# Operands for the second half made inside the first MLP, decode pages multiplied in halves, and wider spacing of memory-key steps

## The chip, the cores and the metric

The kernel runs on one core of a Trainium2 chip. The metric is device time in microseconds of one execution. The engines named below are TensorE (PE in the profile, with PEld for its weight loads), VectorE (DVE), ScalarE (ACT), GpSimd (POOL, which also issues DMAs) and the DMA issuing queue of SyncE (SP).

## What is computed

One inference step of a one-layer decoder, in fp32, for two groups of rows that share the weights: a prompt of 1024 rows and 8 sample rows that each attend to 8192 cached positions. Cut to what matters here:

```python
# prompt
q, k, v, logf, u, z = mixer_inputs(rmsnorm(xp, g_mix), w_in, b_f, g_sgu_v)
xp = xp + merge_heads(fox_prompt(q, k, v, logf), sgu_prompt(u, z, w_s, b_s), g_att_out, g_sgu_out, w_o)
mk, mv = memory_kv(mem_prompt, g_mem, w_ck, w_cv)                  # 256 memory rows
xp = xp + cross_attend(rmsnorm(xp, g_cross), mk, mv, w_cq, w_co)
xp = xp + conv_ffn(rmsnorm(xp, g_ffn), 0, w_up, conv_w, conv_b, w_down)[0]
# samples: the same, with
att = fox_sample(q, k, v, logf, cache_k, cache_v, cache_logf, page_table)   # 64 pages of 128 rows each
xs = xs + cross_attend(rmsnorm(xs, g_cross), cache_mem_k, cache_mem_v, w_cq, w_co)
# merge_heads: concatenate([rmsnorm(att), rmsnorm(sgu)]) @ w_o
# conv_ffn: h = x @ w_up; width-3 causal convolution over rows; (silu(gate) * val) @ w_down, 2816 columns each
```

## The kernel before

**Matmuls.** Every fp32 operand is split into a high and a low part of a faster matmul type (`split`, L231-236): ACT writes the high part (L232, or L235 with a scale), DVE the low part (L233, or L236). `gemm3` (L269-271) then issues three matmuls for each product. Weights arrive by SP DMAs into `wr` tiles of 512 KB (4 buffers) and are split into `wh` (5 buffers) and `wl` (4). Activations lie in a pool `u` of 18 tiles of 128 x 1024. PSUM has eight banks: four `ba`, two `bb`, one `ms`, one `dv`. The prompt's tiles rotate over `ba` and `bb`, every third on `bb`; the samples use `ms` and `dv`.

**The prompt.** The 1024 rows go through in two halves of 512. The order is: projections, attention of half 0, attention of half 1, then for half 0 and then for half 1: a middle stage ("mid0", "mid1") and an MLP ("ffn0", "ffn1"), then the final norm. The middle stage has three parts. `merge_in` (L908) loads the normed attention and gating rows, and `merge` makes their transposed, scaled and split operands in 8 steps: 4 transposes into a bank (L880), then one split by ACT and DVE. `out_proj` (L960) multiplies with `w_o` and adds into the residual rows (`residual`, L952, a DVE add from PSUM and a square on ACT). Cross-attention begins and the MLP begins with `norm_T` (L1018), which transposes three of the four row blocks first (L1027, split in pieces of 128 x 384) and the fourth later (L1043, pieces of 128 x 128).

The MLP (`ffn`, L1167) works in groups of columns. A group first runs its up-projection tiles: 24 matmuls each, a scaled copy by ACT, two convolution steps by DVE (L1214, L1215), in the second half of the prompt a fix of two columns (L1217), and for each pair a product (L1221) and its split. Then it runs down-projection tiles: for each of two column halves (n = 0, 1) and four row blocks. The last group of `ffn` ends with four such tiles at n = 1, and its residual rows are complete after them. A hook, `late`, is called before the last group's down-projection; in half 0 it only issues the loads of `merge_in(1)`.

**The samples.** A second program runs beside the prompt. `decode` goes through 8 samples. For each it takes 16 key steps (`kstep`: an indirect DMA issued by POOL that gathers 1 MB of key pages into a `kv` tile, L1326, a DVE multiply by the query, L1332, and a DVE reduction, L1336) and 16 value steps (`vstep`, L1385: the value pages, then PE matmuls into `dv`, L1391). There are four `kv` tiles. In the attention phases of the prompt a page's multiply and reduction are cut in `KS` = 2 halves, elsewhere each is one instruction of 128 x 2048. Then `sample_rest` follows: the output projection (`sample_proj`, weights through `kv` tiles, sums in bank `ms`), a norm, the query projection, the cross-attention to each sample's own memory keys (a loop over 8 samples: two broadcast loads of the query, a 1 MB load, two multiplies, L1555, one reduction, L1556), to its memory values, and the samples' MLP.

**What sets the order.** Both programs are Python generators. The prompt yields an estimate of its PE time; the driver at the end adds it up and advances the samples' generator by one step each time the sum has passed `PACE` of the phase (8 in mid0, 8.5 in ffn0, 6.8 in mid1, 2.5 in ffn1, 2.9 for `sample_rest`), unless `held[0]` is set. The instructions so issued are then ordered for each engine by a scheduler with its own estimate of times. Two tools steer it: `behind(engine)` places instructions after the last one of the prompt on that engine, and `tc.high_priority()` puts them ahead. The order of an engine is fixed in the built program; what varies in an execution is only how long each instruction waits.

Of the kernel before, what the change touches and what calls it, by code (L numbers as in the profile page):

```python
# [12 lines left out]
ALU = mybir.AluOpType  # L13
AX = mybir.AxisListType
PSUM = bass.MemoryType.PSUM
ENG = mybir.EngineType
DRAM = bass.MemoryType.DRAM

P = 128
# [10 lines left out]
FF = 2816  # L30
NF = FF // P
NPAGE = 64
EPS = 1e-6
NEG = -1e30
UW = 1024
# [43 lines left out]
def build(nc, tc, ctx, a, phases=None):  # L79
# [1099 lines left out]
    def ffn(hf, xt, ys, late=None):  # L1179
        w0, pv0 = wload(a["w_up"][0], 1024), BK()  # L1180

        def up(out, w, hs, ls, c):
            hv, lv = (w[q].rearrange("p (k c) -> p k c", c=P) for q in range(2))
            gemm3(out, [(hv[:, k, :], lv[:, k, :], hs[k][:, c], ls[k][:, c]) for k in range(8)])

        hs, ls = yield from norm_T(ys, G_FFN, lambda hs, ls, c: up(pv0[:, c], w0, hs, ls, c))
        if hf:

            fix = sm([P, 2 * NF, 2], "fix", 1)
            tap = [gp[:, CW + i * 44 : CW + i * 44 + 44] for i in range(2)]  # L1190
            for c in range(2):
                nc.vector.tensor_tensor(fix[:, :, c], hlast[0][:, :, 1], tap[1 - c], op=ALU.mult)
            t = sm([P, 2 * NF], "fixt", 1)
            nc.vector.tensor_tensor(t, hlast[0][:, :, 0], tap[0], op=ALU.mult)
            nc.vector.tensor_tensor(fix[:, :, 0], fix[:, :, 0], t, op=ALU.add)
        sq = squares()
        f0 = 0
        for gi, gn in enumerate(GROUPS):
            gh, gl = [], []
            for f in range(f0, f0 + gn):  # L1200
                hc2 = []
                for part in range(2):
                    ft = f + part * NF
                    cw = [gp[:, CW + i * 44 + ft : CW + i * 44 + ft + 1] for i in range(3)]
                    cb = gp[:, CB + ft : CB + ft + 1]
                    if ft:
                        w_, pv = wload(a["w_up"][ft], 1024), BK()
                        up(pv, w_, hs, ls, slice(0, 512))
                    else:
                        pv = pv0  # L1210
                    hc = T2()
                    nc.scalar.activation(hc, pv, AF.Identity, bias=cb, scale=cw[2])
                    nc.scalar.activation(hlast[hf][:, ft, :], pv[:, 510:512], AF.Copy)
                    nc.vector.scalar_tensor_tensor(hc[:, 1:], pv[:, :511], cw[1], hc[:, 1:], op0=ALU.mult, op1=ALU.add)  # L1214
                    nc.vector.scalar_tensor_tensor(hc[:, 2:], pv[:, :510], cw[0], hc[:, 2:], op0=ALU.mult, op1=ALU.add)  # L1215
                    if hf:
                        nc.vector.tensor_tensor(hc[:, 0:2], hc[:, 0:2], fix[:, ft, :], op=ALU.add)  # L1217
                    hc2.append(hc)
                    yield 5.2
                nc.scalar.activation(hc2[0], hc2[0], AF.Silu)  # L1220
                nc.vector.tensor_tensor(hc2[1], hc2[1], hc2[0], op=ALU.mult)  # L1221
                q = (f - f0) % 2
                if q == 0:
                    g2, l2 = U([P, 2, 512], F32R), U([P, 2, 512], F32R)
                split(hc2[1], g2[:, q, :], l2[:, q, :])
                gh.append(g2[:, q, :])
                gl.append(l2[:, q, :])
            if late and f0 + gn == NF:
                late()
            for n in range(2):  # L1230
                ws = []
                for k2 in range(0, gn, 2):
                    m = min(2, gn - k2)
                    r0 = (f0 + k2) * P
                    h, l, _ = wload(
                        a["w_down"][r0 : r0 + m * P, n * 512 : (n + 1) * 512].rearrange("(k p) n -> p k n", p=P), m * 512
                    )
                    for q in range(m):
                        ws.append((h[:, q, :], l[:, q, :]))
                for i in range(4):  # L1240
                    tb = slice(i * P, (i + 1) * P)
                    ps = MM()
                    gemm3(ps[:, :512], [(gh[k][:, tb], gl[k][:, tb], ws[k][0], ws[k][1]) for k in range(gn)])
                    if f0 + gn < NF:
                        xs_ = xt[i][:, n * 512 : (n + 1) * 512]
                        nc.vector.tensor_tensor(xs_, ps[:, :512], xs_, op=ALU.add)
                    else:
                        residual(xt, sq, i, n, ps)
                    yield 3.9
            f0 += gn  # L1250
        if hf:
            nc.sync.dma_start(a["o_h"], hlast[1])
        return sq
# [20 lines left out]
    def decode():  # L1274
# [48 lines left out]
        def kstep(b, ch, st):  # L1323
            qb, s = st
            kv = KV()
            nc.gpsimd.indirect_dma_start(kv, None, a["cache_k"], off(kidx[:, b, ch : ch + 1]))  # L1326
            kvv = kv.rearrange("p (k c) -> p k c", c=512)
            sp = KS if phase[0][:3] == "att" else 1
            m = 4 // sp
            with behind(ENG.DVE):  # L1330
                for i in range(0, 4, m):
                    nc.vector.tensor_tensor(  # L1332
                        kvv[:, i : i + m, :], kvv[:, i : i + m, :], qb.unsqueeze(1).broadcast_to((P, m, 512)), op=ALU.mult
                    )
                for i in range(0, 4, m):
                    nc.vector.tensor_reduce(  # L1336
                        s[:, ch * 4 + i : ch * 4 + i + m, :].rearrange("p k h -> p (k h)"),
                        kvv[:, i : i + m, :].rearrange("p k (h d) -> p (k h) d", d=64),
                        axis=AX.X,
                        op=ALU.add,  # L1340
                    )
# [138 lines left out]
    def sample_out(n, ps, fin):  # L1480
        t = D2()
        nc.scalar.activation(t, ps, AF.Copy)
        yield 1
        ps2 = MS()
        mmul(ps2[:8, :], selS, t, start=True, stop=True)
        fin(n, ps2[:8, :])

    def sample_proj(w, xT, fin):
        for n in range(2):
            ps = MS()  # L1490
            for kk in range(4):
                if kk % 2 == 0:
                    raw = KV().rearrange("p (k n) -> p k n", n=512)
                    nc.gpsimd.dma_start(raw, w[kk * 256 : (kk + 2) * 256, n * 512 : (n + 1) * 512].rearrange("(k p) n -> p k n", p=P))
                    yield 1
                sample_mm(ps, raw[:, (kk % 2) * 2 : (kk % 2) * 2 + 2, :], kk, xT, 512)
            yield from sample_out(n, ps, fin)

    def sample_rest(xs):
        yield 1  # L1500
# [45 lines left out]
        for b in range(8):  # L1546
            qb = [D2(), D2()]
            for n in range(2):
                nc.gpsimd.dma_start(qb[n], q2s_d[b : b + 1, n * 512 : (n + 1) * 512].broadcast_to((P, 512)))
            kv = KV()  # L1550
            nc.gpsimd.dma_start(kv.rearrange("p (a c) -> p a c", c=D), a["cmk"][b].rearrange("(a p) c -> p a c", p=P))
            kvv = kv.rearrange("p (a c) -> p a c", c=D)
            for n in range(2):
                kn = kvv[:, :, n * 512 : (n + 1) * 512]
                nc.vector.tensor_tensor(kn, kn, qb[n].unsqueeze(1).broadcast_to((P, 2, 512)), op=ALU.mult)  # L1555
            nc.vector.tensor_reduce(sS[:, :, b, :], kv.rearrange("p (a h d) -> p a h d", a=2, h=4), axis=AX.X, op=ALU.add)  # L1556
            yield 1
        yield 1
        tr = MS()
        for mt in range(2):  # L1560
# [160 lines left out]
    def prompt():  # L1721
# [2 lines left out]
            if not G0R:  # L1724
                yield from gating(0)

        got = []
        att1 = attention(1, lambda: got.append(merge_in(0)))
        att0, fill0 = attention(0, (lambda: next(att1)) if LT < 4 else None, LT), fill()

# [27 lines left out]
        next(ending)  # L1758
        ends = []
        for hf in range(2):  # L1760
            if not got:
                got.append(merge_in(hf))
            xt = []
            phase[0] = f"mid{hf}"
            mh, ml = yield from beside(merge(*got.pop()), ending, (3, 7)) if hf == 0 else merge(*got.pop())
            if ends:
                yield from ends.pop()
            sq = yield from out_proj(a["w_o"], mh, ml, xt, partial(load_x, hf))
# [2 lines left out]
            else:  # L1771
                ys = yield from cross(xt, sq)
            phase[0] = f"ffn{hf}"
            sq = yield from ffn(hf, xt, ys, (lambda: got.append(merge_in(1))) if LM and hf == 0 else None)
            ends.append(final(hf, xt, sq))
        yield from ends.pop()

# [8 lines left out]
    for t in prompt():  # L1786
# [8 lines left out]
        while bgs and not held[0] and most and acc[0] >= PACE[phase[1] or phase[0]]:  # L1795
            most -= 1
            acc[0] -= PACE[phase[1] or phase[0]]
            if next(bgs[0], None) is None:
                bgs.pop()
        seen = len(nc.cur_bb.bb.instructions)  # L1800
    for _ in bgs.pop() if bgs else ():
        pass
# [90 lines left out]
```

## Time and profile before

| | |
|---|---|
| median of 3 runs | 1905.01 us (1898.7 to 1908.0) |
| the profiled execution | 1899.86 us, its span 1898.1 us |
| PE busy | 1817.0 us (96%), 9255 matmuls |
| VectorE busy | 1394.5 us (73%), 1574 instructions |
| ScalarE busy | 755.7 us (40%) |
| GpSimd busy | 490.6 us (26%) |
| moved by DMA | 517.06 MB, mean 272 GB/s |
| mean granted TensorE clock | 0.979 |

The profile's times count from the start of the span. The middle stage of half 0 lies around 545 to 780 us, its MLP from there to 1166, the middle stage of half 1 from 1166 to about 1410, and its MLP from there to the end. The loop over the samples' memory keys lies at 1573 to 1635. "Idle before" is the time an engine sat with nothing to do ahead of an instruction, and the name behind the arrow is what ended that time.

### The profile page before, as it was taken

To read this page: it belongs to the slowest core of one execution; us is meant where nothing else is said; L and a number is where in the kernel's file an instruction comes from. 1 tells how busy PE (TensorE), PEld (TensorE's weight loads), DVE (VectorE), ACT (ScalarE), POOL (GpSimd) and SP (SyncE) were. 2 spreads that over 40 slices of the span, in tenths; PEclk is the share of its full clock that TensorE was granted. 3 is DMA by queue.
4 is the path that set the end of the run, shared out by engine and by line. 5 is a ranking of instruction groups with operands and counts; after the bars stand their busy time and mean duration, and the time that the engine had idled before them with its cause. 6 is when DMAs were issued, how large, how long until landed. Compare 5 with 4: busy or idle time off the path is not lost.

```text
span 1898.1 us, 24082 instructions
## 1 busy us (share of the span) xinstructions
PE 1817.0 (96%) x9255; PEld 1299.4 (68%) x9255; DVE 1394.5 (73%) x1574; ACT 755.7 (40%) x1371; POOL 490.6 (26%) x429
## 2 busy tenths in 40 slices
PE   8999999788899999999999999998999999999998
PEld 5987666555676667777767776775675667667765
DVE  4888678776678786989989998888764548754344
ACT  5332356565633534424233243325353333232332
POOL 1342242222122332313431322344222012101110
PEclk9999999989999999999999999999999999999999
DMA  8867988853397875869878879888859557666872
GB/s 320 292 246 278 324 319 292 280 168 126 136 376 251 337 274 214 310 229 353 307 266 311 309 298 348 340 337 300 308 218 356 198 200 271 226 223 255 323 275 101
DMA packets 156371, 517.06 MB, mean 272 GB/s; under 512 B 20168, under 2 KB 41928, under 8 KB 123488
## 3 DMA queue, kind: packets, MB, share of 16 engines
q0 software_dynamic: 56400, 339.04, 48.0%
q1 hardware_dynamic: 92944, 163.89, 24.8%
q10 hardware_dynamic: 6912, 12.59, 1.8%
q8 instruction: 73, 1.20, 0.2%
q14 instruction: 42, 0.34, 0.0%
HBM read 493.63 MB, written 21.84 MB: 272 GB/s over the span
## 4 chain that ended last, share of the span: by engine, by line
PE 82%; DVE 8%; ACT 4%; DMA 3%; issue 2%; POOL 0%; SPq 0%; DVEq 0%; POOLq 0%; ACTq 0%
PE ba L270 12%; PE ba L269 12%; PE ba L271 12%; PE bb L269 7%; PE bb L270 7%; PE bb L271 7%; PE dv L1391 6%; DVE kv L1332 2%; DMA kv<-cache_k,kidx 1%; PE dv L1634 1%; PE bb L795 1%; PE ba L993 1%; PE ba L994 1%; PE ba L995 1%; DVE wl L233 1%
## 5 line engine op out<-in xcount | busy, mean ns | idle before, releaser
L232 ACT ACTIVATE wh<-wr 128x1024 fp32r<-128x1024 f32 (+2 forms) x220 | 228.7, 1044 | 483.0 <-PE ba L270 154.6
L233 DVE TENSOR_TENSOR wl<-wr,wh 128x1024 fp32r<-128x1024 f32 (+2 forms) x220 | 262.6, 1200 | 155.4 <-PE ba L271 70.2
L1326 POOL DMA_INDIRECT kv<-cache_k,kidx x128 | 185.7, 1451 | 528.6 <-DVE s L1336 241.7
L1332 DVE TENSOR_TENSOR kv<-kv,d 128x2048 f32<-128x2048 f32 (+1 forms) x139 | 292.4, 2114 | 34.9 <-DMA kv<-cache_k,kidx 34.0
L1336 DVE TENSOR_REDUCE s<-kv 128x32 f32<-128x2048 f32 (+1 forms) x139 | 292.2, 2106 | 0.7
L1385 POOL DMA_INDIRECT kv<-cache_v,kidx x128 | 182.5, 1426 | 403.5 <-DVE s L1336 196.1
L269 PE MATMUL ba<-wh,u 128*128 128x512 f32 (+1 forms) x596 | 227.0, 382 | 0.0
L270 PE MATMUL ba<-wl,u 128*128 128x512 f32 (+1 forms) x596 | 226.2, 380 | 0.0
L271 PE MATMUL ba<-wh,u 128*128 128x512 f32 (+1 forms) x596 | 223.1, 379 | 0.7 <-DVE u L233 0.7
L269 PE MATMUL ba<-u,wh 128*128 128x512 f32 (+2 forms) x520 | 203.6, 392 | 1.2 <-DVE u L236 1.2
L270 PE MATMUL ba<-u,wh 128*128 128x512 f32 (+2 forms) x520 | 204.1, 393 | 0.0
L271 PE MATMUL ba<-u,wl 128*128 128x512 f32 (+2 forms) x520 | 202.9, 390 | 0.0
L1391 PE MATMUL dv<-kv,s 128*32 128x512 f32 x1024 | 138.2, 614 | 5.5 <-DMA kv<-cache_v,kidx 5.5
L269 PE MATMUL bb<-u,wh 128*128 128x512 f32 (+2 forms) x344 | 137.7, 400 | 0.0
L270 PE MATMUL bb<-u,wh 128*128 128x512 f32 (+2 forms) x344 | 136.4, 397 | 0.0
L271 PE MATMUL bb<-u,wl 128*128 128x512 f32 (+2 forms) x344 | 135.4, 395 | 0.0
L269 PEld LDWEIGHTS ba<-wh,u 128*128 128x128 f32 x596 | 112.5, 189 | 31.9 <-issue 8.0
L271 PEld LDWEIGHTS ba<-wh,u 128*128 128x128 f32 x596 | 111.8, 188 | 28.6 <-issue 6.3
L270 PEld LDWEIGHTS ba<-wl,u 128*128 128x128 f32 x596 | 112.5, 189 | 24.6 <-issue 3.8
L270 PEld LDWEIGHTS ba<-u,wh 128*128 128x128 f32 x520 | 98.7, 190 | 32.8 <-issue 12.6
L269 PEld LDWEIGHTS ba<-u,wh 128*128 128x128 f32 x520 | 98.8, 190 | 31.8 <-issue 7.1
L271 PEld LDWEIGHTS ba<-u,wl 128*128 128x128 f32 x520 | 98.6, 190 | 28.5 <-issue 9.3
(416 smaller groups left out, 3080.5 us busy)
## 6 DMA issues: line engine op xcount, KB each, us to landing
wr<-w_up SPq DMA_DIRECT2D x88, 512.0 KB
kv<-w_up POOLq DMA_DIRECT2D x22, 1024.0 KB
wr<-w_down SPq DMA_DIRECT2D x40, 512.0 KB
kv<-w_down POOLq DMA_DIRECT2D x11, 1024.0 KB
wr<-w_in SPq DMA_DIRECT2D x16, 512.0 KB
wr<-w_o SPq DMA_DIRECT2D x16, 512.0 KB
wr<-w_cq SPq DMA_DIRECT2D x16, 512.0 KB
wr<-w_co SPq DMA_DIRECT2D x16, 512.0 KB
```

What stands on the lines that cost most here:

```text
L232: nc.scalar.activation(h, src, AF.Copy)
L233: nc.vector.tensor_tensor(l, src, h.bitcast(F32), op=ALU.subtract)
L269: mmul(out, sh, mh, start=(i == 0), stop=False)
L270: mmul(out, sh, ml, start=False, stop=False)
L271: mmul(out, sl, mh, start=False, stop=(i == n - 1))
L795: mmul(po[64 * j : 64 * j + 64, q0:256], vn[:, kt, 64 * j : 64 * j + 64], pt[j][kt // 4][:, kt % 4, q0:256], start=(kt == 0), stop=(kt == ...
L993: mmul(pss[i], mh[k][:, tb], wh, start=(k == korder[0]), stop=False)
L1326: nc.gpsimd.indirect_dma_start(kv, None, a["cache_k"], off(kidx[:, b, ch : ch + 1]))
L1332: nc.vector.tensor_tensor(kvv[:, i : i + m, :], kvv[:, i : i + m, :], qb.unsqueeze(1).broadcast_to((P, m, 512)), op=ALU.mult)
L1336: nc.vector.tensor_reduce(s[:, ch * 4 + i : ch * 4 + i + m, :].rearrange("p k h -> p (k h)"), kvv[:, i : i + m, :].rearrange("p k (h d) -> ...
L1385: nc.gpsimd.indirect_dma_start(kv, None, a["cache_v"], off(kidx[:, b, ch : ch + 1]))
L1391: mmul(dv[32 * j : 32 * j + 32, :], s[:, ch * 4 : ch * 4 + 4, :].rearrange("p k h -> p (k h)"), kvv[:, j, :], start=(ch == 0), stop=(ch == ...
```

## The change

Five things change.

1. The hook `late` of `ffn` in half 0 now returns the generator `merge(1)` (its loads are issued at the same place as before). After each of the four last down-projection tiles (last group, n = 1) two of its 8 steps are run. From the first of these on `held[0]` is set, so the samples' program rests until `ffn` returns. Half 1 then takes the finished operands and goes straight on to the final norm of half 0 and to `out_proj`.
2. A page's multiply and reduction are cut in halves in mid0 and mid1 too.
3. `sample_proj` uses bank `dv` for its first column half and `ms` for the second, and issues both halves' matmuls before either half's sums.
4. The loop over memory keys puts its DVE instructions `behind(DVE)`, cuts the reduction in two, and yields `CMK` = 3 instead of 1; the driver charges that step three times.
5. The load of `merge_in(hf)` at the head of the loop is limited to half 0.

In the new file lines from the MLP's hook on stand one to some twenty lines further down (L880 becomes L881).

```diff
+CMK = 3
...
+            side = None
             if late and f0 + gn == NF:
-                late()
+                side = late()
...
                     yield 3.9
+                    if side and n:
+
+                        held[0] = True
+                        for _ in range(2):
+                            yield next(side)
...
-            sp = KS if phase[0][:3] == "att" else 1
+            sp = KS if phase[0][:3] in ("att", "mid") or held[0] else 1
...
-        ps2 = MS()
+        ps2 = (DV, MS)[n]()
...
     def sample_proj(w, xT, fin):
+        outs = []
         for n in range(2):
-            ps = MS()
+            ps = (DV, MS)[n]()
...
-            yield from sample_out(n, ps, fin)
+            outs.append(sample_out(n, ps, fin))
+            next(outs[n])
+        for o in outs:
+            yield from o
+        yield 1
...
-            for n in range(2):
-                kn = kvv[:, :, n * 512 : (n + 1) * 512]
-                nc.vector.tensor_tensor(kn, kn, qb[n].unsqueeze(1).broadcast_to((P, 2, 512)), op=ALU.mult)
-            nc.vector.tensor_reduce(sS[:, :, b, :], kv.rearrange("p (a h d) -> p a h d", a=2, h=4), axis=AX.X, op=ALU.add)
-            yield 1
+            with behind(ENG.DVE):
+                for n in range(2):
+                    kn = kvv[:, :, n * 512 : (n + 1) * 512]
+                    nc.vector.tensor_tensor(kn, kn, qb[n].unsqueeze(1).broadcast_to((P, 2, 512)), op=ALU.mult)
+                for i in range(2):
+                    nc.vector.tensor_reduce(sS[:, i, b, :], kvv[:, i, :].rearrange("p (h d) -> p h d", h=4), axis=AX.X, op=ALU.add)
+            yield CMK
...
-            if not got:
+            if not got and hf == 0:
...
-            mh, ml = yield from beside(merge(*got.pop()), ending, (3, 7)) if hf == 0 else merge(*got.pop())
+            if hf == 0:
+                mh, ml = yield from beside(merge(*got.pop()), ending, (3, 7))
+            else:
+                mh, ml = yield from ahead[0]
...
-            sq = yield from ffn(hf, xt, ys, (lambda: got.append(merge_in(1))) if LM and hf == 0 else None)
+            sq = yield from ffn(hf, xt, ys, (lambda: ahead.append(merge(*merge_in(1))) or ahead[0]) if hf == 0 else None)
+            held[0] = False
...
-            if next(bgs[0], None) is None:
+            w = next(bgs[0], None)
+            if w is None:
                 bgs.pop()
+            else:
+                acc[0] -= (w - 1) * PACE[phase[1] or phase[0]]
```

More of the change, by code (lines that the diff above doesn't have):

```diff
@@ L1725, in fill @@
                 yield from gating(0)
-        got = []
+        got, ahead = [], []
         att1 = attention(1, lambda: got.append(merge_in(0)))
```

## The prediction

> **What bounds the kernel now.** I read the page first, then the PE waits, then windows over the places where PE waited.
>
> ```profile
> span 1898.1 us, 24082 instructions
> PE 1817.0 (96%) x9255; PEld 1299.4 (68%) x9255; DVE 1394.5 (73%) x1574; ACT 755.7 (40%) x1371; POOL 490.6 (26%) x429
> PE 82%; DVE 8%; ACT 4%; DMA 3%; issue 2%; POOL 0%; SPq 0%; DVEq 0%; POOLq 0%; ACTq 0%
> ```
>
> PE is busy for 1817.0 of 1898.1 us, and 82% of the chain that ended last is PE. So 81 us of idle PE, start and end included, is nearly all that a change of order can win, beside matmuls that ran at a lowered clock. The PE waits say for whom PE sat idle (us in total, times, longest):
>
> ```profile
> PE bb L269 <- DVE t L1217: 6.4, 1, 6.4
> PE dv L1391 <- DMA kv<-cache_v,kidx: 5.5, 2, 3.6
> PE ba L880 <- DVE u L952: 3.8, 1, 3.8
> PE ba L1043 <- DVE u L236: 3.8, 2, 1.9
> PE ba L1027 <- DVE u L236: 3.3, 2, 2.2
> PE bb L1027 <- DVE u L952: 2.9, 2, 2.5
> ```
>
> In the second half of the kernel PE mostly waits for VectorE, and in single pieces of 2 to 6 us. The windows place them. Columns: us, then busy time of PE, PEld, DVE, ACT and POOL (instructions), the granted clock, DMA share, GB/s.
>
> ```profile
> 586.20:588.30 2.10, 0.24 (x2) 0.12 (x1) 2.10 (x5) 0.00 (x0) 0.00 (x0) 0.93 0.36 152
> 588.00:591.40 3.40, 3.22 (x12) 2.86 (x13) 3.40 (x5) 0.63 (x2) 0.00 (x0) 0.50 0.03 5
> 1169.90:1173.90 4.00, 0.20 (x3) 0.07 (x2) 4.00 (x6) 2.45 (x7) 2.47 (x2) 1.00 1.03 414
> 1175.00:1178.50 3.50, 3.50 (x19) 2.63 (x12) 3.50 (x5) 1.59 (x3) 0.94 (x1) 0.51 0.99 372
> 1231.70:1240.50 8.80, 5.71 (x35) 5.09 (x32) 8.80 (x13) 2.28 (x5) 3.52 (x2) 1.00 0.95 381
> 1310.90:1323.00 12.10, 6.50 (x23) 3.45 (x21) 8.95 (x10) 5.85 (x17) 1.88 (x2) 0.72 0.95 381
> 1610.20:1616.80 6.60, 0.22 (x2) 0.13 (x1) 6.60 (x8) 1.14 (x2) 0.71 (x1) 0.89 0.84 295
> 1616.00:1622.50 6.50, 5.80 (x14) 4.64 (x15) 6.50 (x9) 1.17 (x2) 0.00 (x0) 0.52 0.55 209
> ```
>
> Read them in pairs. From 1169.90 to 1173.90 DVE is busy without pause while PE does 0.20 us, and from 1175.00 the clock is 0.51 for 3.5 us. The pair at 1610 is the largest: PE does 0.22 of 6.60 us, then runs at 0.52 for another 6.5 us. A gap of under 2 us near 587 is followed by the same 0.50, while the two gaps inside 1231.70 to 1240.50 leave the clock at 1.00. So a lost microsecond of PE can cost up to two.
>
> [...]
>
> **The change part by part.** *Memory-key steps of the samples* (spacing of three, held behind DVE's last main instruction, reductions in halves). This stretch now:
>
> ```profile
> 1577.00:1632.00 55.00, 47.87 (x195) 37.96 (x194) 54.93 (x56) 16.43 (x26) 10.49 (x17) 0.94 0.76 262
> L1555 DVE TENSOR_TENSOR kv<-kv,d 128x1024 f32<-128x1024 f32 x16 | 19.3, 1218 | 4.7 <-DMA d<-q2s_d 4.7
> L1556 DVE TENSOR_REDUCE sS<-kv 128x8 f32<-128x2048 f32 x8 | 18.2, 2277 | 0.0
> L233 DVE TENSOR_TENSOR wl<-wr,wh 128x1024 fp32r<-128x1024 f32 x9 | 10.9, 1216 | 0.0
> L1214 DVE SCALAR_TENSOR_TENSOR t<-ba,gp,t 128x511 f32<-128x511 f32 x4 | 3.0, 743 | 0.0
> L1221 DVE TENSOR_TENSOR t<-t,t 128x512 f32<-128x512 f32 x4 | 2.7, 684 | 0.0
> ```
>
> DVE is full for 55 us. Its own 24 instructions take 19.3 + 18.2 = 37.5 us, about 36 at the spacing of starts (a record overlaps the next by some 0.08). An up-projection tile asks DVE for a weight split (1.14 by starts), two convolution steps (0.66 each), a small fix, and half of a gate product and its split (0.60 each): about 3.1 us. Seven such tiles and two weight splits for the next group make 36 + 22 + 2 = 60 us of DVE. Seven tiles are 7 x 24 matmuls, 0.23 us apart (starts 1159.64, 1159.86, 1160.09 below), so 39 us of PE. DVE falls 21 us behind. PE sat idle for 55 - 47.87 = 7.1 of it, so buffers absorbed about 14. After the change eleven tiles stand between the first and the last memory-key step: DVE 36 + 11 x 3.1 = 70, PE 11 x 5.5 = 61. The 9 us of lag left is below the 14 that buffers absorbed. What can go is 7.1 of gap and the lowered clock behind it, 14 matmuls in 5.80 us at 1616, 0.41 each instead of 0.23: 2.6: together 9.7. I take -8.5, since at the turn from up- to down-projection tiles the margin is only about 1 us. Bounds: -10 (all), and 0 if the lag just moves there. The cover for the decode steps is PE's lead; if it is gone, the same 7 us come back. Splitting eight reductions adds 8 x 0.07 = 0.6 of DVE, inside the lag. The steps come later, but the steps after them take up the delay: behind the samples' last DVE instruction stand 24 of the prompt's, where 19 stood, so the end isn't lengthened.
>
> *Second half's operands between the last down tiles of the first MLP.*
>
> ```profile
> 1156.61 0.69 DVE L952 TENSOR_TENSOR u<-ba,u 128x512 f32<-128x512 f32 x1
> 1157.22 2.28 DVE L1332 TENSOR_TENSOR kv<-kv,d 128x2048 f32<-128x2048 f32 x1
> 1159.42 0.68 DVE L952 TENSOR_TENSOR u<-ba,u 128x512 f32<-128x512 f32 x1
> 1160.02 0.68 DVE L952 TENSOR_TENSOR u<-bb,u 128x512 f32<-128x512 f32 x1
> 1168.57 2.27 DVE L1336 TENSOR_REDUCE s<-kv 128x32 f32<-128x2048 f32 x1
> 1170.76 2.35 DVE L233 TENSOR_TENSOR wl<-wr,wh 128x1024 fp32r<-128x1024 f32 x2
> 1173.09 0.68 DVE L952 TENSOR_TENSOR u<-ba,u 128x512 f32<-128x512 f32 x1
> 1159.64 0.39 PE L269 MATMUL ba<-wh,u 128*128 128x512 f32 x1
> 1159.86 0.39 PE L270 MATMUL ba<-wl,u 128*128 128x512 f32 x1
> 1160.09 0.39 PE L271 MATMUL ba<-wh,u 128*128 128x512 f32 x1
> ```
>
> Today PE reaches the transposes at 1169.9 and waits 3.80 us for a residual add (L952) that stands on DVE behind a page reduction and two weight splits. The same 32 transposes, 32 scalings and residual adds are issued afterwards; none is saved. In pairs of four they now stand between tiles of 15 matmuls (3.5 us of PE), in which ACT and DVE split them. That cover holds for the later pairs. The first pair needs a bank that a residual add frees. In the new DVE order that add stands behind another add and a full page multiply: starts 0.61 + 2.20 + 0.60 apart, 3.4 us, against about 1.4 of PE work in front of it by the new PE order (two matmuls and a group of page matmuls, an estimate), so a new wait of about 2.0; the last tile may wait 0.8 for its add, a little more than one add takes. So 3.80 goes and 2.8 comes; with the lowered clock at 1175 gone (3.5 us at half rate, of which I count 1.3 as lost), and a half chance of 1.5 for a drop behind the new wait, that is -1.0 - 1.3 + 0.75 = -1.5. Bounds: -5 (both stalls gone) and +2 (both new waits with a clock drop, no old cost saved but half). On SP, three loads of the output projection's weights now stand behind g_final and four x loads; those wait for buffers that PE's tiles free. At 1169.9 DMA share is 1.03, so a late load is possible; I cost it at 0, hidden behind the remaining tiles, and up to +2 without that cover. Decode is held for about 16 us of yielded work, and afterwards goes on one step per main step until it has caught up; its instructions are in the same places again before cross-attention. Price 0; if not, see the second rival.
>
> *Pages in halves in the mid stages.* 45 more pages become four instructions.
>
> ```profile
> L1332 DVE TENSOR_TENSOR kv<-kv,d 128x2048 f32<-128x2048 f32 x117 | 266.6, 2283 | 34.9 <-DMA kv<-cache_k,kidx 34.0 <-PE bb L1126 0.7
> L1332 DVE TENSOR_TENSOR kv<-kv,d 128x1024 f32<-128x1024 f32 x22 | 25.8, 1215 | 0.0
> 1235.56 2.28 DVE L1336 TENSOR_REDUCE s<-kv 128x32 f32<-128x2048 f32 x1
> 1237.75 2.28 DVE L1332 TENSOR_TENSOR kv<-kv,d 128x2048 f32<-128x2048 f32 x1
> 1240.03 0.60 DVE L236 SCALAR_TENSOR_TENSOR u<-ba,gp,u 128x128 fp32r<-128x128 f32 x2
> ```
>
> Two halves take 2 x 1215 - 2283 = 147 ns more by duration; by starts about 0.07 per pair, two pairs a page: 45 x 0.14 = 6 us more DVE work over the two mid stages. It costs PE nothing unless DVE is awaited. Halves only help if something is ordered between them. In the new order, at the waits near 575, 586 and 737, the two halves still stand together ahead of the awaited scaling, so these stay. Near 1238 the multiply of 2.28 us, which stood ahead of the scalings at 1240.03, now stands behind the first two: the 1.9 us wait ends 2.2 us earlier and goes. Take -2. Bounds: -8 (every one of those waits halved, with its clock drop) to +4 (each of about five gets 0.14 to 0.3 longer, and one more drop).
>
> *Samples' projections* (two PSUM buffers in turn): PE has no wait in these stretches now, so 0, within 1 either way.
>
> Sum: -8.5 - 1.5 - 2 = -12.0 on the profiled execution's 1899.86, so 1887.9. That execution is 5.15 below the median of 1905.01; on the median I forecast 1893.0.
>
> **The rivals.** (a) *The samples' lag moves rather than goes.* The memory-key steps run on into the turn to the down-projection, where DVE must free banks for tiles of fewer matmuls; about 7 us of idle PE return and the parts above give only 3: 1905 - 12 + 8.5 = 1901.5. For it: margin of 1 us there, DVE at 54.93 of 55. Against: 14 us absorbed now.
>
> (b) *Slower: pages late in the second mid stage.* The one wait of this kind now is in the row from 1310.90: PE does 6.50 of 12.10 us at a clock of 0.72, so 5.6 idle and some 2.6 slowed, 8 us for one late V page. Holding decode for 16 us and then issuing a step at each main step bunches page loads where DMA share is already 0.95 to 1.03. Each such page beyond today's adds 8 to the 1893: one gives 1901, two 1909, three 1917. From the second on the change loses; I price the rival at three, 1917. Against it: the queues' order of page loads is nearly the same, and PE waited for cache_v only twice in the whole execution (the second row of the waits).
>
> (c) *That late V page disappears.* Ahead of it stands a long POOL issue:
>
> ```profile
> 1294.47 0.94 POOL L1385 DMA_INDIRECT kv<-cache_v,kidx  x1 [0.30 <-PE ba L1100]
> 1296.46 9.07 POOL L1326 DMA_INDIRECT kv<-cache_k,kidx  x1 [1.05 <-DVE s L1336]
> ```
>
> Its neighbour took 0.94 us. If DVE's work beside it held it up, shorter DVE instructions may let it through, and then the 8 us go too: 1885. [...]
>
> (d) *The halves do nothing*, since the planner keeps them adjacent: 1895; part of my forecast's range.
>
> **How the numbers follow.** Forecast 0.47 (alone 1887 to 1899), (a) 0.19, (b) 0.18, (c) 0.16. A difference under 0.5% (9.5 us) is about what measurement can't tell from none. Faster by more: all of (c) and four fifths of the forecast, 0.54. Within: (a) and the rest of the forecast, 0.28. Slower: (b) at three pages or more, 0.18. The range of 8 in 10 runs from 1881, (c) with its bounds, to 1910, past (a) and up to two late pages of (b).
>
> **What would show it.** The 6.4 us wait of L269 for t L1217 should be gone, with the clock at 1.00 there, and the memory-key steps spread over some 60 to 75 us. The transposes of L880 (L881 then) should stand between tiles, with one PE wait near 2 us before them in place of 3.80. The waits at 575, 586 and 737 should be as before; that near 1238 should be gone. I am wrong if PE's waits for DMA in the second mid stage grow, if a wait of 3 us or more appears at the MLP's turn, or if PE's idle time falls by 12 us and the span doesn't.

## The result and the profile after

The changed kernel takes 1883.97 us (median of 7 runs, 1881.13 to 1890.86) where the kernel before takes 1904.38 us (7 runs, 1895.84 to 1909.6). The ratio is 0.9903, with a 95% interval of 0.9884 to 0.9923: 15 to 22 us faster. In a later comparison it was 0.9929 (0.9913 to 0.9945). The two profiled executions differ by less, 1899.86 against 1887.23 us. The head of the page of after:

```profile
span 1885.5 us, 24204 instructions
PE 1810.9 (96%) x9255; PEld 1298.5 (69%) x9255; DVE 1400.3 (74%) x1672; ACT 755.7 (40%) x1371; POOL 478.6 (25%) x429
PE 84%; DVE 6%; DMA 4%; ACT 3%; issue 2%; POOL 1%; SPq 0%; DVEq 0%; POOLq 0%; ACTq 0%
```

VectorE does 6 us more work, as the halves ask (1400.3 against 1394.5). PE's busy time falls by 6 us with the same 9255 matmuls; fewer of them at a lowered clock would do that (behind the 6.38 us wait of before they start 0.43 us apart, at full clock 0.23), but the mean granted clock of the two executions, 0.979 and 0.980, is too coarse to show it. PE's waits in after (us in total, times, longest), the ones that answer to the list before:

```profile
PE dv L1398 <- DMA kv<-cache_v,kidx: 5.5, 2, 3.6
...
PE ba L1028 <- DVE u L237: 5.0, 4, 2.2
...
PE bb L1028 <- DVE u L953: 3.3, 2, 2.5
PE ba L270 <- DVE u L953: 2.7, 2, 2.5
...
PE bb L1044 <- DVE u L237: 2.2, 1, 2.2
...
PE bb L271 <- DVE u L237: 1.5, 1, 1.5
```

The wait of 6.4 us for t L1217 is gone. The 3.8 us before the transposes is gone, and a wait of 2.5 for a residual add (L953 now) has come. The waits of norm_T and the matmuls behind it for the scalings (L237) did not shrink: 5.0, 2.2 and 1.5 us here, 3.8 and 3.3 in the rows before. Two windows of after, columns as in the prediction:

```profile
1550.00:1612.00 62.00, 62.00 (x271) 50.59 (x270) 61.87 (x75) 22.31 (x40) 10.49 (x18) 1.00 0.73 249
1174.00:1178.50 4.50, 4.50 (x26) 2.93 (x25) 4.50 (x7) 3.85 (x6) 2.56 (x1) 1.00 0.85 294
```

In the first, which holds most of the memory-key loop of after (1550.6 to 1617.8), DVE is as full as before (61.87 of 62) and PE does not pause once, at full clock. The second lies behind the new 2.53 us wait: the clock stayed at 1.00.

### The profile page after: what moved, and what is told of

The parts are those of the page before. It is cut to its first block, busy times and chain, and to the rows that moved or that the text cites. A ratio compares the mean times of both kernels' runs of the same rounds, so it can differ in the third digit from the quotient of the medians.

```text
span 1885.5 us, 24204 instructions
## 1 busy us (share of the span) xinstructions
PE 1810.9 (96%) x9255; PEld 1298.5 (69%) x9255; DVE 1400.3 (74%) x1672; ACT 755.7 (40%) x1371; POOL 478.6 (25%) x429
## 4 chain that ended last, share of the span: by engine, by line
PE 84%; DVE 6%; DMA 4%; ACT 3%; issue 2%; POOL 1%; SPq 0%; DVEq 0%; POOLq 0%; ACTq 0%
PE ba L270 13%; PE ba L271 13%; PE ba L272 12%; PE bb L270 7%; PE bb L271 7%; PE bb L272 7%; PE dv L1398 6%; DVE kv L1339 1%; PE dv L1648 1%; DVE s L1343 1%; PE bb L796 1%; PE ba L994 1%; PE ba L996 1%; PE ba L995 1%; DMA wr<-w_ck 1%
## 5 line engine op out<-in xcount | busy, mean ns | idle before, releaser
L1339 DVE TENSOR_TENSOR kv<-kv,d 128x1024 f32<-128x1024 f32 (+1 forms) x184 | 295.5, 1634 | 27.3 <-DMA kv<-cache_k,kidx 27.1
L1333 POOL DMA_INDIRECT kv<-cache_k,kidx x128 | 175.0, 1367 | 552.8 <-DVE s L1343 257.6
L1343 DVE TENSOR_REDUCE s<-kv 128x16 f32<-128x1024 f32 (+1 forms) x184 | 296.6, 1626 | 0.2
L270 PE MATMUL ba<-wh,u 128*128 128x512 f32 (+1 forms) x601 | 229.7, 384 | 3.1 <-DVE u L953 2.7
L270 PE MATMUL ba<-u,wh 128*128 128x512 f32 (+2 forms) x520 | 204.4, 394 | 0.4 <-DVE u L237 0.4
L270 PE MATMUL bb<-u,wh 128*128 128x512 f32 (+2 forms) x344 | 138.6, 403 | 0.7 <-DVE u L237 0.7
L270 PEld LDWEIGHTS ba<-wh,u 128*128 128x128 f32 x601 | 113.3, 189 | 37.6 <-issue 10.7
L270 PEld LDWEIGHTS ba<-u,wh 128*128 128x128 f32 x520 | 99.3, 191 | 31.4 <-issue 8.4
```

The costliest lines, as they stand in the source:

```text
L270: mmul(out, sh, mh, start=(i == 0), stop=False)
L1339: nc.vector.tensor_tensor(kvv[:, i : i + m, :], kvv[:, i : i + m, :], qb.unsqueeze(1).broadcast_to((P, m, 512)), op=ALU.mult)
L1343: nc.vector.tensor_reduce(s[:, ch * 4 + i : ch * 4 + i + m, :].rearrange("p k h -> p (k h)"), kvv[:, i : i + m, :].rearrange("p k (h d) -> ...
```

## The experiments

**How the stages are read.** Single traces carry noise: from the start to the fifth residual add the built order is the same in the ten kernels whose pages are whole in mid0, and yet this stretch took 551.4 to 557.4 us in their traces. (In the four with halves in mid0 a few pages of this stretch are already in halves; they took 555.4 to 558.1.) So I cut each trace at four instructions of the prompt: the fifth residual add (L952), the first convolution step of the first MLP (L1214), its 41st, and the first convolution step of the second MLP; the last cut is the last scaling of the final norm. Kernels with the same edit in a stage stand together. In mid0, in the first MLP and, where the table does not say otherwise, around mid1 their orders of instructions are the same, so they are replicas; in the second MLP they differ in places. All numbers in us, from the starts of those instructions:

| stage | edit in force there | traces | time, mean | lowest to highest |
|---|---|---|---|---|
| mid0 | pages whole | 10 | 206.3 | 205.5 to 207.4 |
| | pages in halves | 4 | 209.8 | 209.1 to 211.5 |
| first MLP, to its 41st up tile | any | 14 | 358.2 | 358.2 to 358.3 |
| from there through mid1 | merge behind the MLP, whole | 4 | 299.4 | 298.2 to 300.1 |
| | merge behind, halves (two orders) | 2 | 299.1 | 298.6 to 299.5 |
| | merge inside, decode held, whole | 2 | 295.6 | 295.2 to 296.0 |
| | merge inside, held, halves in mid0 and mid1 | 3 | 293.3 | 291.6 to 295.8 |
| | merge inside, held, halves in mid1 only | 2 | 290.2 | 289.3 to 291.1 |
| | merge inside, not held, halves in mid1 only | 1 | 287.7 | |
| second MLP | loop and projections as before | 3 | 477.6 | 477.4 to 478.0 |
| | loop alone changed | 1 | 476.3 | |
| | projections alone changed | 1 | 475.8 | |
| | both, spacing of one | 1 | 474.4 | |
| | both changed | 8 | 467.2 | 465.1 to 469.5 |

The changed kernel is by this +3.5 in mid0, -6.1 around mid1 and -10.4 in the second MLP: -13.0. The second measured ratio is -13.5 us, the first -18.5.

**The memory-key loop alone.** To the kernel before (the comments stand for lines of the change that are left out here):

```diff
+CMK = 3
-            for n in range(2):                 # two multiplies, one reduction
+            with behind(ENG.DVE):              # two multiplies, two half reductions
...
-            yield 1
+            yield CMK
...
+            else:
+                acc[0] -= (w - 1) * PACE[phase[1] or phase[0]]
```

> The kernel before with one part of the change alone: the loop over memory keys spaced by three, its DVE instructions held behind the prompt's, its reductions in halves. My theory (the lag of DVE is absorbed by PE's lead): the wait of 6.4 us of L269 for t L1217 goes with its lowered clock, 9 to 11 us faster, ratio 0.994 to 0.9955. Rival (the lag moves to the turn to the down-projection tiles): a wait of 4 us or more appears there, at most 3 us faster, ratio 0.998 or more.

Measured: 0.9985 (0.9971 to 0.9998), so 0.4 to 5.5 us, and the rival's number. The wait is still there. First a row of its PE waits, then a window over it:

```profile
PE bb L270 <- DVE t L1218: 5.1, 1, 5.1
```

```profile
1612.00:1626.00 14.00, 8.86 (x30) 6.77 (x29) 14.00 (x17) 2.97 (x5) 1.27 (x2) 0.76 0.71 274
```

The built order tells why: between the first and last step still lie seven up tiles, as before, and the loop still ends at the turn to the down-projection. The spacing could not stretch it. My theory, that this edit alone gives room, falls.

**The samples' projections alone, and both.** To the kernel before (the second kernel has the edit above as well):

```diff
-            ps = MS()
+            ps = (DV, MS)[n]()
...
-            yield from sample_out(n, ps, fin)
+            outs.append(sample_out(n, ps, fin))
+            next(outs[n])
+        for o in outs:
+            yield from o
+        yield 1
```

> The kernel before with the samples' projections alone changed (two PSUM banks in turn, both halves' matmuls first); the memory-key loop as before. By the built order the loop then starts three up tiles earlier in its MLP group and has four up tiles behind it before the turn, in place of none, and six between its steps in place of seven. Theory L (the place of the loop decides: the lag is paid back before the turn): the wait of 6.4 us goes without any spacing, ratio 0.994 to 0.996. Theory S (the spacing decides too): 21 us of lag in six tiles are still more than the buffers absorb, a wait of 4 us or more stays earlier in the group, ratio 0.998 to 1.000.

> The kernel before with the projections and the memory-key loop both changed, nothing else. By the built order ten up tiles lie between the first and the last step. Both theories: the wait goes, ratio 0.993 to 0.9955; theory L expects no difference to the projections alone, theory S 6 us or more between them. If it gains less than 4 us, the rest of the change is needed too and both fall.

The projections alone: 0.9994 (0.9978 to 1.001), no difference. Both: 0.9951 (0.9932 to 0.997). Theory S has the right ratios and L falls, though the wait of 4 us or more that S placed earlier in the group did not come: two edits that are each worth 1 to 2 us in the second MLP's stage are worth 10 together. With the projections alone the loop starts at 1556.8 in place of 1572.1, PE goes through it without a pause, and the loss comes behind it. Two windows, and PE's timeline (start, busy time, then idle before and who ended it):

```profile
1556.00:1607.00 51.00, 51.00 (x223) 41.61 (x222) 50.84 (x52) 17.54 (x31) 10.47 (x18) 1.00 0.79 268
1607.00:1630.00 23.00, 19.23 (x71) 14.31 (x70) 21.70 (x35) 11.34 (x18) 1.43 (x2) 0.85 0.58 211
```

```profile
1616.40 0.40 PE L1566 MATMUL ms<-cp,sS 128*32 128x128 f32 x2 [2.08 <-DVE sS L1561]
1618.19 0.79 PE L269 MATMUL bb<-wh,u 128*128 128x512 f32 x1 [1.40 <-DVE t L1215]
```

The steps are issued closely, so the samples' own transposes of the finished scores (L1566) stand in PE's order before VectorE has worked off the reductions, and PE waits for them with all up tiles behind; then the lag shows as a second wait. With the spacing as well, the same loop spreads over 1551.0 to 1621.1, ten up tiles instead of six:

```profile
1551.00:1616.00 65.00, 65.00 (x284) 52.96 (x283) 64.97 (x81) 24.09 (x41) 11.03 (x18) 1.00 0.75 257
```

DVE is full, and so is PE. The traces show a second thing that the projections change. In the four kernels without that edit DVE itself sits idle for 4.4 to 5.4 us before steps at the head of the loop, until the loads of the query land (2.16 and 2.56 us in the kernel before); in the ten with it this takes 0.4 us at most. How much of the pair's gain is this and how much the earlier start, no run separates.

**The spacing back to one in the changed kernel.**

```diff
-CMK = 3
+CMK = 1
```

> The changed kernel with the memory-key steps spaced by one again (still behind DVE's main work and in halves). Theory L: same as the changed kernel within 2 us, ratio to before 0.990 to 0.992. Theory S: 5 us or more slower than the changed kernel, ratio 0.993 or more, with a wait of 3 us or more between the up tiles.

Measured: 0.9973 (0.9959 to 0.9987). The second MLP takes 474.4 in place of 467.2 us, the same loss from the other side. Theory S again; its wait was not one of 3 us but four of 0.7 to 1.5, two of them again for the score transposes.

**The merge alone.** To the kernel before: the hook returns `merge(1)`, two steps after each last tile, decode held.

```diff
+                    if side and n:
+                        held[0] = True
+                        for _ in range(2):
+                            yield next(side)
```

> The kernel before with the second half's operands made between the first MLP's last tiles and decode held there, nothing else. Theory: the wait of 3.8 us before the transposes goes, one of about 2.5 us stays, the clock drop behind it goes: 2 to 5 us faster, ratio 0.9975 to 0.999. Rival (the hold bunches page loads in mid1 and a page comes late): no gain or up to 8 us slower, ratio 1.000 to 1.004, with a longer wait of L1391 or L1332 for its page.

Measured: 0.9971 (0.9957 to 0.9985), 3 to 8 us, about the upper end of what I expected. The wait of 3.8 us is gone and one of 2.54 stands there, with no clock drop behind it in this trace (three of the seven traces with this wait have one). The stage around mid1 is 3.9 shorter than with the merge behind (two traces against four). No page came clearly later than in the kernels without it: the wait for a V page near 1311 was 3.3 to 5.7 us in those and 4.7 and 5.2 in these two.

**The halves alone, and the change without them.**

```diff
-            sp = KS if phase[0][:3] == "att" else 1
+            sp = KS if phase[0][:3] in ("att", "mid") else 1
```

> The kernel before with pages cut in halves in mid0 and mid1, nothing else. Theory from the two traces: mid0 loses 4 us, because two scalings of norm_T fall behind a page multiply that waits for its page (a new PE wait near 600 us), and mid1 wins back at most 2: 2 to 4 us slower, ratio 1.001 to 1.002. Rival (halves shorten what PE waits for, and their loss in mid0 comes from another part): 2 to 6 us faster, ratio 0.997 to 0.999.

> The changed kernel with pages whole again in mid0 and mid1. Theory (halves cost 4 us in mid0): 2 to 4 us faster than the changed kernel, ratio to before 0.988 to 0.9895, with mid0's end within 0.5 us of before. Rival (the halves are needed where decode catches up in mid1): 2 us or more slower than the changed kernel, ratio 0.9915 or more, with waits in mid1 grown.

Halves alone: 1.0006 (0.999 to 1.0022), undecided by time, though mid0 is longer (209.1). Without halves: 0.9918 (0.9899 to 0.9937); the changed kernel's 0.9903 lies inside that interval. So over the kernel the halves balance. In mid0 they cost 3.5 us, and the trace of after shows where. First, near 580, half of a page's reduction stands between scalings that PE waits for, where the whole reduction stood behind them. DVE, PE, and the window behind:

```profile
578.54 1.21 DVE L1343 TENSOR_REDUCE s<-kv 128x16 f32<-128x1024 f32 x1
579.67 0.61 DVE L237 SCALAR_TENSOR_TENSOR u<-bb,gp,u 128x384 fp32r<-128x384 f32 x1
```

```profile
580.33 0.69 PE L270 MATMUL bb<-u,wh 128*128 128x384 f32 x1 [0.71 <-DVE u L237]
```

```profile
578.10:584.90 6.80, 6.09 (x21) 5.57 (x22) 6.14 (x13) 2.10 (x3) 1.97 (x2) 0.50 0.83 288
```

In both kernels the clock is lowered to 0.50 behind the wait ahead of this one (2.18 us in the kernel before, 2.25 here), but in the kernel before it is back at 1.00 from 581.20, after 3.4 us. All four traces with halves have this wait (0.70 or 0.71 us) and the 6.8 us at half clock, none of the ten with whole pages. It puts PE 2.2 us back: the same later matmul (L269 before, L270 in after) starts at 584.38 in the kernel before and at 586.94 here, where the fifth residual add lies 0.36 later. Then, near 600, DVE and PE again:

```profile
595.73 0.34 DVE L237 SCALAR_TENSOR_TENSOR u<-bb,gp,u 128x128 fp32r<-128x128 f32 x1
598.36 2.36 DVE L1339 TENSOR_TENSOR kv<-kv,d 128x1024 f32<-128x1024 f32 x2 [2.29 <-DMA kv<-cache_k,kidx]
600.64 0.35 DVE L237 SCALAR_TENSOR_TENSOR u<-ba,gp,u 128x128 fp32r<-128x128 f32 x1
600.90 0.34 DVE L237 SCALAR_TENSOR_TENSOR u<-bb,gp,u 128x128 fp32r<-128x128 f32 x1
```

```profile
601.30 0.33 PE L271 MATMUL bb<-u,wh 128*128 128x128 f32 x1 [1.46 <-DVE u L237]
```

The planner put the two halves of a multiply ahead of the last two scalings. On the chip their page came late, so DVE sat idle for 2.29 us with the scalings queued behind, and PE waited for them. In the kernel before, that multiply stands behind all of them. This wait is 1.2 to 1.5 us in the four traces with halves.

**Halves in mid1 only, twice, beside the changed kernel again.** To the changed kernel:

```diff
-            sp = KS if phase[0][:3] in ("att", "mid") or held[0] else 1
+            sp = KS if phase[0][:3] == "att" or phase[0] == "mid1" else 1
```

> The changed kernel with pages in halves in the attention phases and mid1, whole in mid0. If the halves cost 3 to 4 us in mid0 and win 3 us in mid1, as the two runs with and without halves seem to say, this is 2 to 4 us faster than the changed kernel: ratio to before 0.988 to 0.990. If halves do nothing that can be told, 0.990 to 0.992.

> Halves in the attention phases and mid1 only, once more. By the stages 3.1 us faster than the changed kernel from mid0 (about 206 us instead of 209.3), and mid1 the same: ratio to before 0.9885 to 0.991. If it is no faster than the changed kernel here, the cost of halves in mid0 is noise of single traces.

> The changed kernel once more, on one chip with the three below. Stages of the traces so far (mid0 +3.1, end of the first MLP and mid1 -8, second MLP -10.5 against kernels with the same orders as before) sum to -15.5: ratio to before 0.9905 to 0.993. If something outside those stages gained too, 0.989 or less again.

Measured: 0.9889 (0.9865 to 0.9912), then 0.9906 (0.989 to 0.9922) beside 0.9929 (0.9913 to 0.9945) for the changed kernel. On that chip its median is 1882.32 against 1886.38 us. Mid0 gives back its loss (205.5 and 207.2 against 209.3 and 211.5), and mid1, which this edit also puts in another order, is shorter too (290.2 against 293.3); the intervals of the ratios still overlap, so that it beats the changed kernel is likely and not certain.

**The place of the merge, and the hold, with halves in mid1 only.** The first leaves `held[0] = True` out; the second runs `merge` at the start of mid1:

```diff
-                        held[0] = True
```

```diff
-                side = late()
+                late()
```

> The same with halves in mid1 only, but decode not held between the last tiles of the first MLP. Theory (the hold keeps page multiplies out of the way of the residual adds): the wait before the merge grows past 2.5 us or a second one appears, the stage from the first MLP's last tiles to the second MLP 2 to 5 us longer than with the hold. Rival (the hold only bunches pages later): no difference, or up to 3 us shorter, with the wait of L1398 for its page shorter.

> The same with halves in mid1 only, but the merge of the second half run at the start of mid1, after the MLP, as in the kernel before; no hold. Theory (the place of the merge is worth about 4 us whatever else is changed): the wait of 3.8 us before the transposes returns, 4 us slower than with the merge inside. Rival (merge and halves in mid1 only gain together): 7 us or more slower, the stage back at 299 us.

Without the hold: 0.9897 (0.9879 to 0.9915), no slower than with it. The wait at the merge was 1.53 us in place of 2.53, against my theory, and the V page's wait 0.51 us in place of 1.3 and 1.5, as the rival had it:

```profile
1170.26 0.50 PE L270 MATMUL ba<-wh,u 128*128 128x512 f32 x1 [1.53 <-DVE u L953]
```

Holding decode bought nothing here; whether leaving it out gains, the runs do not settle. With the merge behind the MLP: 0.9953 (0.9938 to 0.9968), 1889.93 us against 1882.32; the stage is back at 298.6 and the 3.8 us wait is back. This is the rival: merge and halves in mid1 gain together. Halves without the merge gave 0.3 us there, the merge without halves 3.9, both 9.2 in this order; in the order of the changed kernel both gave 6.1, which single traces can hardly tell from the sum.

## Why the prediction was right, and where its steps were not

The forecast of 1893.0 was 9 us above the median, inside the range of 1881 to 1910 and on the right side of zero. It is outside the 1887 to 1899 that the forecast claimed for its own mechanism, and nearest to rival (c)'s 1885, whose late page did not go. The sum, -12.0, agrees with the two profiled executions (-12.6) and with the stages (-13.0). That is in part luck: the terms missed by about -2, -2.5 and +3, and these nearly cancel.

- **Memory-key loop, -8.5.** Its size was nearly right (-10.4, past the bound of -10), and so was its picture: DVE full, PE's lead enough. I had counted eleven tiles between the first and the last step; the trace of after has nine. By the same working that leaves a lag of 36 + 9 x 3.1 - 9 x 5.5 = 14 us, just what I had said the buffers absorb. The attribution failed. I read the spread from an order in which the projections were changed too, and gave the gain to the spacing. The step that failed is "Samples' projections: PE has no wait in these stretches now, so 0". They have no wait of their own on PE; they decide when the loop begins (1550.6 in place of 1572.1), and so whether the spacing has tiles to spread over before the turn, and they end DVE's own wait for the query's loads. Without them the lag stays where it was; without the spacing it comes out behind the loop, at the samples' own transposes on PE, a wait I had not thought of.
- **Merge, -1.5.** Mis-sized: -3.9 alone. 3.80 us went with its lowered clock, as worked out; of the 2.8 of new waits 2.5 came, but as one wait of a later tile. The chain I walked was the wrong one. DVE's rows before that wait in after:

```profile
1169.16 1.21 DVE L1315 TENSOR_TENSOR_SCAN d<-rmask,d 128x512 f32<-128x512 f32 x1
1170.29 2.25 DVE L1343 TENSOR_REDUCE s<-kv 128x32 f32<-128x2048 f32 x1
1172.46 0.68 DVE L953 TENSOR_TENSOR u<-ba,u 128x512 f32<-128x512 f32 x1
```

  The add stood behind a scan and a page reduction of the held decode's last step, not behind a multiply. The half chance of a clock drop, for which I had added 0.75, was about right: no drop followed in this trace, but in three of the seven traces with this wait one did, a second trace of the changed kernel among them.
- **Halves, -2.** The sign was right in mid1 and missed in mid0. I said the waits near 575, 586 and 737 stay, and they did (2.25, 2.19, 2.45 us); the wait near 1238 fell from 1.91 to 0.36 us, as worked out, though the clock, at 1.00 there before, was at 0.50 from 1233.5 for 3.4 us. What the step left out are the new orders near 580 and near 600, which make up the +3.5. "It costs PE nothing unless DVE is awaited" was the sentence at fault: half a page's work can move ahead of awaited scalings (PE's wait of 0.71 us at 580), and a page multiply that nobody awaits can wait for a DMA with awaited work behind it (2.29 us on DVE, 1.46 on PE near 600). In mid1 the gain with the merge inside was about 2 in the changed kernel's order (293.3 against 295.6, three traces against two, whose ranges overlap), and I have no single wait that shows it.
- **Rivals.** (a), the lag that only moves, is what each part of the pair did alone. (b), late pages, did not come: 3.60 us for the V page near 1315 against 3.64. (c) came in part: the long GpSimd issue near 1300 took 6.87 us in place of 9.07.

```profile
1301.32 6.87 POOL L1333 DMA_INDIRECT kv<-cache_k,kidx  x1 [1.71 <-DVE s L1343]
```

  In both traces of halves in mid1 only, with the merge inside and decode held, the V page's wait was down to 1.3 and 1.5 us; in the two traces of the changed kernel it was 3.6 and 4.2. DVE's rows beside the issue near 1300 in after:

```profile
1301.65 2.32 DVE L234 TENSOR_TENSOR wl<-wr,wh 128x1024 fp32r<-128x1024 f32 x2
1303.90 2.34 DVE L1339 TENSOR_TENSOR kv<-kv,d 128x1024 f32<-128x1024 f32 x2
1306.17 1.21 DVE L234 TENSOR_TENSOR wl<-wr,wh 128x1024 fp32r<-128x1024 f32 x1
1307.31 1.20 DVE L1343 TENSOR_REDUCE s<-kv 128x16 f32<-128x1024 f32 x1
```

  The TENSOR_TENSOR rows, two splits, two multiplies and a split, follow each other without a break until 1307.38, and the issue ends at 1308.19, 0.81 us later. In the kernel before, a run of them with a scan of 1.20 us in it ends at 1304.72 and the 9.07 us issue at 1305.53, again 0.81 later. Of the 83 indirect issues over 1.2 us in that trace, 68 end 0.80 to 0.84 us behind the end of a DVE TENSOR_TENSOR, and none does behind a TENSOR_REDUCE. In these two rows, then, the issue's end follows the end of a run and not that of one instruction, and halves need not shorten a run: with halves and the merge behind the MLP the issue took 9.14 us. That the run holds the issue up is my reading; no run changed this alone.
- **The sum and the median.** The sum was set against a profiled execution 5 us under the median of its kernel. The gap between -12 and the first ratio's -18.5 is not found in any stage: the stages give -13.0, a second comparison -13.5, and the first 550 us vary by 6.0 in an identical order. What made the first comparison larger stays open.

## What to carry to other kernels

When two programs share engines, look at where a stretch of background work lies against the main program's stages, not only at how densely it is issued: an edit that only moves the start of such a stretch can be the condition for another edit to work at all. Cutting an instruction in halves invites the planner to move it, and it may move ahead of awaited work; read the new order for what stands behind an instruction that waits for a DMA, and for halves that now stand between awaited pieces. Where one trace against one trace must settle a few microseconds, use the stretches in which other variants have the same order as replicas.

## What the runs showed of the hardware

- The time of an identical order varied by 6.0 us over the first 550 us (551.4 to 557.4 in ten traces), while the 358.2 us of the first MLP up to its 41st up tile, where PE never waits, agreed within 0.2 us in 14.
- The length of a PE gap of 2 to 3 us did not tell whether the clock drops. In after, 2.53 us at 1170.7 left it at 1.00 (the window above), and 2.25 us at 575.8 was followed by the 6.8 us at 0.50 shown under the halves. The same wait of 2.53 us in another execution of the changed kernel was followed by this:

```profile
1175.50:1178.90 3.40, 3.40 (x8) 2.72 (x9) 3.40 (x6) 1.62 (x4) 1.22 (x2) 0.50 0.63 212
```

  In all, a drop followed this wait in three of seven traces, and the wait of 3.80 us in six of six. Why one and the same wait goes either way, no run shows.
- The long GpSimd DMA issue near 1300 ended 0.81 us behind the end of a run of DVE TENSOR_TENSOR instructions, in the traces of before and after alike. It took 9.07 us in each of the six traces with whole pages in mid1, and 6.87 or 6.88 us in the three with the changed kernel's order there: the order repeats to 0.01 us what it costs.
